# Moving steps in four written-out lists, one fixed sequence for a reciprocal root, and an early Silu, in an encoder block on one core

## Chip, cores and metric

The kernel runs on one core of one Trainium2 chip. Its time is the device time of one launch in microseconds (us). Three runs were made of it; the number that counts is their median.

## What is computed

One layer of an encoder on 256 tokens of width 2048, in float32. h = RMSNorm(x) goes through one projection that gives queries, keys and values of three token mixers A, B and C and three gates of width 2048. Each mixer's result goes through its own branch projection; the gates merge the three; an output projection w_o and a residual add follow; then a SwiGLU feed-forward (FFN) of inner width 5632.

```python
h = rms_norm(x, g_mix)
proj = h @ w_in                      # q, k, v of A and B, q of C, 3 gates
oa, ob, oc = dilated_attention(...), grouped_query_attention(...), cross_attention(mem, ...)
gates = sigmoid(gt)
merged = gates[0] * (oa @ w_br_a) + gates[1] * (ob @ w_br_b) + gates[2] * (oc @ w_br_c)
x = x + merged @ w_o
hf = rms_norm(x, g_ffn) @ w_ffn_in
x = x + (silu(hf[..., :D_FF]) * hf[..., D_FF:]) @ w_ffn_out
```

## The kernel before, in words

**Products in two halves.** Every weight block is a tile of 128 x 1024 float32 ("raw", 512 KB, one DMA of SP's queue, issued in `load`, L207). ScalarE rounds it to the matmul type (the high half, `whi`, L418), VectorE subtracts that from the block (the low half, `wlo`, L428), and each product is three matmuls: high by high, high by low, low by high. All matmuls are recorded at L79, where a helper issues them.

**Stages.** First the projection of the memory tokens and eight projections of q, k and v (`product`), with the attention worked between them as side jobs; then gates and branches (`merging`, pairs of 512 columns), the output projection (`projecting`) and the FFN (`feeding`), in which eleven pairs of hidden columns alternate with the pairs of the second FFN matrix. From `merging` on, all pairs run as one stream through `run(everything(), 4)`.

**A pair and its steps.** `pair` computes two 512-column blocks (c = 0 and 1) for 256 tokens (two halves t = 0 and 1). For most of the inner dimension it uses a scheme with seven products in place of eight (`seventh`, L537). Its four sums stand in four PSUM banks, called Y and X (c = 0) and W and Q (c = 1); in the first gate pair (`early`) a bank V takes the place of X as a result. The steps of a pair are written out by hand as a string:

- l and r load the blocks of one double step (`begin`, `begin2`); `begin` loads b11 and t and has GpSimd's queue (POOL, L503) add a further block into t.
- X, W, P, Y, Q, Z, H are the seven products, 6 matmuls each, with the number of the double step behind the letter (0 or 1). X adds to bank X, W and Z to bank W, Y to bank Y, P and Q to bank X again, H to X (or V). P, Q and H first make their block on VectorE (L549, L551, L553).
- d and D are plain products over a whole block of 256 inner rows, for c = 0 (banks Y and X, or V) and c = 1 (banks W and Q): 12 matmuls.
- A dot takes one step from the list that the pair before has left over.

Each entry has three lists: front (with dots), back, and the left-over end that goes to the next pair.

**The turning points of the chain** are in `phase_end` (L514): when the last X is done, ScalarE copies bank X into Y (L526); when the last W is done, ScalarE copies bank W away as m5 (L529); when the last P is done, VectorE writes W = m5 - X (L531); when the last Q is done, VectorE writes Q = m5 - X (L535), and in the `early` pair ScalarE first copies X to `u` (L521) and VectorE adds it to V (L522).

**What sets the order.** `run` prepares four steps ahead of the one whose matmuls it issues: a step's `ready` issues its load, its block sum, its high half and (one step later, `low(1)`) its low half; `products` issues its matmuls. The matmuls and SP's DMAs keep program order. `nc.follow` puts an instruction behind the one that was last given to it on the same engine, so the high halves on ScalarE and the low halves, block sums and bank operations on VectorE each form one fixed sequence. An engine works through its own queue in order, so an instruction that waits holds those behind it. Whatever is not given to `nc.follow` is placed by the planner, which simulates the program and takes what is ready, by priority. Side jobs are generators which `tick` moves on after every step's products, one at most each time; `urgent` gives theirs a high priority.

**The reciprocal root.** `row_scale` (L153) turns a row's sum of squares into r = 1/sqrt(mean + eps): one `tensor_scalar` (L156), then `rsqrt` (L138) with a shift and a subtraction on the bits (L142, L143) and three Newton rounds of three operations (L147 to L149), then a copy (L158) and a square (L159). In `projecting` the job `later` (L910) squares the sums on ScalarE (L914) and, at the last of four column blocks, reduces them (L918) and calls `row_scale` for r_f. The first use of r_f is the scale of the Silu of the first FFN pair (`hidden`, L947). That Silu reads banks W and Q, which the next pair's W0 needs.

**Activation tables.** ScalarE loads a table before the first function that is not in the one that it has: at the start (L338, a copy on the two-column tile `two`), before the first Sigmoid (L814) and before the first Silu (L947).

Of the kernel before, what the change touches and what calls it, by code (L numbers as in the profile page):

```python
# [13 lines left out]
I32 = mybir.dt.int32  # L14
AF = mybir.ActivationFunctionType
ALU = mybir.AluOpType
AX = mybir.AxisListType
# [4 lines left out]
D = 2048  # L22
# [9 lines left out]
EPS = 1e-6  # L32
# [19 lines left out]


STEPS_GATE = [
# [3 lines left out]
STEPS_O = ("l0 X0 . r0 W0 . P0 Y0 . Q0 .", "Z0 D2 H0 D3 d2 D6 d3 D7 D4 D5", "d6 d7 d4 d5")  # L58
STEPS_O2 = ("l0 X0 . r0 W0 . P0 Y0 . Q0 .", "Z0 D2 H0 D3 d2 D4 D5 d3 D6 D7", "d4 d5 d6 d7")
STEPS_FFN0 = ("l0 l1 X0 X1 . r0 W0 . r1 W1 . P0 P1 . Y0 Y1 Q0 Q1", "Z0 Z1 D6 H0 D7 H1 D4 D5", "d6 d7 d4 d5")  # L60
STEPS_FFN = ("l0 l1 X0 X1 . r0 W0 r1 W1 P0 P1 . Y0 Y1 . Q0 Q1 .", "Z0 Z1 D4 H0 D5 H1 D6 D7", "d4 d5 d6 d7")
STEPS_LAST = ("l0 l1 X0 X1 . r0 W0 . r1 W1 . P0 P1 . Y0 Y1 Q0 Q1", "Z0 Z1 H0 H1 D4 D5", "d4 d5")
STEPS_LAST2 = ("l0 l1 X0 X1 . r0 W0 r1 W1 P0 P1 . Y0 Y1 Q0 Q1", "Z0 Z1 D4 H0 D5 H1 d4 d5", "")


class InOrder:
# [37 lines left out]
def encoder_block(ctx: ExitStack, tc: tile.TileContext, a: dict, out: bass.AP):  # L104
    nc = InOrder(tc)
# [13 lines left out]
    def s8(shape, name, dt=F32R, pool=None):  # L119
        return (pool or big).tile(shape, dt, name=name, tag="s8")  # L120

    def s4(shape, name, dt=F32):
        return mid.tile(shape, dt, name=name, tag="s4")
# [14 lines left out]
    def rsqrt(v, shape):  # L138

        y = small.tile(shape, F32, name="rs_y")  # L140
        h = small.tile(shape, I32, name="rs_h")
        nc.vector.tensor_scalar(h, v.bitcast(I32), 1, None, op0=ALU.logical_shift_right)  # L142
        nc.vector.tensor_scalar(y.bitcast(I32), h, -1.0, float(0x5F3759DF), op0=ALU.mult, op1=ALU.add)  # L143
        for _ in range(3):
            t = small.tile(shape, F32, name="rs_t")
            y2 = small.tile(shape, F32, name="rs_y")
            nc.vector.scalar_tensor_tensor(t, y, -0.5, y, op0=ALU.mult, op1=ALU.mult)  # L147
            nc.vector.tensor_mul(t, t, v)
            nc.vector.scalar_tensor_tensor(y2, t, 1.5, y, op0=ALU.add, op1=ALU.mult)  # L149
            y = y2  # L150
        return y

    def row_scale(ss, r):  # L153

        v = small.tile([P, T], F32, name="rs_v")
        nc.vector.tensor_scalar(v, ss, 1.0 / D, EPS, op0=ALU.mult, op1=ALU.add)  # L156
        y = rsqrt(v, [P, T])
        nc.vector.tensor_copy(r[:, 0], y)  # L158
        nc.vector.tensor_mul(r[:, 1], y, y)  # L159


    side, now = [], [0]
# [11 lines left out]
    def start(steps):  # L174

        job = [0, steps]
        side.append(job)
        advance(job)
# [7 lines left out]
    def urgent(steps):  # L186

        while True:
            with tc.high_priority():
                try:  # L190
                    lag = next(steps)
                except StopIteration:
                    return
            yield lag
# [91 lines left out]
    def transposed(src, dst, g=None, lag=1, also=None):  # L286


        full = None
        for h in range(2):  # L290
            if h:
                yield lag
            tp = bank("tp", "tp")
            for k in range(2):
                for t in range(T):
                    nc.tensor.transpose(tp[:, k * S + t * P:k * S + (t + 1) * P],
                                        src[t][:, (2 * h + k) * P:(2 * h + k + 1) * P], ident)
            if g is None:
                d = dst(2 * h, 2)
                split(d[0], d[1], tp.rearrange("p (k s) -> p k s", s=S))  # L300
            else:
                for k in range(2):
                    d = dst(2 * h + k, 1)
                    split(d[0], d[1], tp[:, k * S:(k + 1) * S], g(2 * h + k))
            if also is not None:
                if full is None:
                    full = s4([P, 2, 4, P], "ffull")
                to, of = full[:, :, 2 * h:2 * h + 2], tp.rearrange("p (k t s) -> p k t s", t=T, s=P)
                if g is None:
                    nc.scalar.activation(to, of, AF.Copy)  # L310
                else:
                    for k in range(2):
                        nc.scalar.activation(to[:, k], of[:, k], AF.Copy, scale=g(2 * h + k))
        if also is not None:
            token_sums(full, also)
# [20 lines left out]
    two = const.tile([P, 2], F32, name="two")  # L336
# [288 lines left out]
    def take_slots(ps, slots, r, name="x"):  # L625
# [22 lines left out]
        if n:  # L648
# [4 lines left out]
            nc.vector.tensor_mul(ss[:, :, :n], ss[:, :, :n], each(1))  # L653
            nc.vector.tensor_scalar(v[:, :, :n], ss[:, :, :n], 1.0 / HD, EPS, op0=ALU.mult, op1=ALU.add)
            nc.vector.tensor_mul(f[:, :, :n], rsqrt(v[:, :, :n], [P, T, n]), each(0))
            yield EVAC_LAG
            for t in range(T):
# [178 lines left out]
    ss1 = const.tile([P, T, 4], F32, name="ss1")  # L836
# [55 lines left out]
    def projecting():  # L892
        def rows():
            yield 16
            for t in range(T):
                x.append(s8([P, D], f"x{t}", F32))
                nc.sync.dma_start(out=x[t], in_=a["x"][t * P:(t + 1) * P, :])
                yield 1
        start(rows())
        mTl = lambda k: (mT[k // 4][:, 0, k % 4], mT[k // 4][:, 1, k % 4])  # L900
        ended = []
        for n in (0, 2):
            def add(c, r, n=n):
                xc = [x[t][:, (n + c) * NC:(n + c + 1) * NC] for t in range(T)]
                for t in range(T):
                    nc.vector.tensor_add(xc[t], r[t], xc[t])
                ended.append(n + c)
                last = len(ended) == 4

                def later():  # L910
                    yield 1
                    sq = s4([P, T, NC], "sq")
                    for t in range(T):
                        nc.scalar.activation(sq[:, t], xc[t], AF.Square, accum_out=ss1[:, t, n + c:n + c + 1])  # L914
                    if last:
                        yield 1
                        ssr = small.tile([P, T], F32, name="ss", bufs=1)
                        nc.vector.tensor_reduce(ssr, ss1, axis=AX.X, op=ALU.add)  # L918
                        row_scale(ssr, r_f)
                    yield 2  # L920
                    if not x1T:
                        x1T.extend(s8([P, 2, 4, S], "x1T") for _ in range(4))
                        room.extend(form_room(3))
                    yield from transposed(xc, lambda k, m: (x1T[n + c][:, 0, k], x1T[n + c][:, 1, k]),
                                          lambda k: gT[:, 2, 4 * (n + c) + k:4 * (n + c) + k + 1], 2,
                                          also=room[2 + n + c] if n == 0 else None)
                start(urgent(later()))
            yield pair(block_pair(a["w_o"], n), mTl, STEPS_O2 if n else STEPS_O, add, TWO[:1], by_room(lambda: room))
# [6 lines left out]
    def feeding():  # L935
        for c0, c1 in ((0, 4), (4, 8), (8, KF // 4)):
# [3 lines left out]
            for n in range(c0, c1):  # L940
                av = []

                def hidden(c, v, av=av, n=n - c0, hT=hT):
# [8 lines left out]
                    def later():  # L952
                        tl = hT[n] = s8([P, 2, 4, S], "hT", pool=home(n))
                        yield 3
                        yield from transposed([av[0][:, t] for t in range(T)],
                                              lambda k, m: (tl[:, 0, k:k + m], tl[:, 1, k:k + m]), lag=2,
                                              also=room[n] if n < 2 else None)
                    start(urgent(later()))
                yield pair(lambda u, c, n=n: a["w_ffn"][n][2 * u + 1 - c], x1l, STEPS_FFN if n else STEPS_FFN0, hidden,
                           TWO, by_room(lambda: room[2:]))  # L960
            pairs = (STEPS_LAST, STEPS_LAST2) if last else (STEPS_FFN, STEPS_FFN)
            for n in (0, 2):
# [105 lines left out]
```

## Time and profile before

| | us |
|---|---|
| three runs | 1372.01, 1372.15, 1373.7 |
| median | 1372.15 |
| the profiled execution | 1372.53 |
| its span, first to last instruction | 1370.8 |
| TensorE busy in it | 1356.7 (99%) |
| VectorE busy | 1156.3 (84%) |
| ScalarE busy | 856.8 (63%) |
| table loads, starting at | 1.2, 283.6, 714.6 |

The granted clock of TensorE over the whole execution was 0.997. Two kinds of views are used below. Timeline rows tell when an instruction started, how long it took, its engine (PE is TensorE, DVE VectorE, ACT ScalarE), its line, what it writes and reads, and in square brackets how long the engine was idle before it and what ended that. Window rows tell, for a stretch of time, how long each engine was busy, how many instructions that were, and the granted clock.

### The profile page before, as it was taken

How to read it: one execution, taken by the hardware profiler on the slowest of the kernel's cores; microseconds unless marked ns; L12 is line 12 of the kernel's file. 1: busy time of each engine (PE TensorE's matmuls, PEld its weight loads, DVE VectorE, ACT ScalarE, POOL GpSimd, SP SyncE). 2: the span in 40 equal slices, each digit the busy share in tenths (PEclk: the TensorE clock that was granted, in tenths of full speed). 3: DMA queues.
4: the chain of work that ended last, by engine and by line, in shares of the span. 5: the costliest groups of instructions: out<-in, count | busy, mean ns of one | idle time of the engine just before them, and what ended most of it. 6: DMA issues, size and time to landing. Idle time of an engine off the chain costs nothing.

```text
span 1370.8 us, 17289 instructions
## 1 busy us (share of the span) xinstructions
PE 1356.7 (99%) x6170; PEld 1122.8 (82%) x6170; DVE 1156.3 (84%) x1412; ACT 856.8 (63%) x1110; POOL 53.2 (4%) x60
## 2 busy tenths in 40 slices
PE   9999999998999999999999999999999999999998
PEld 7878888887878888888878888888888888888887
DVE  6878877767879779878888998889999889989997
ACT  7776666655656556656666666655666656566664
POOL 0010000000000000000000000000000000000000
PEclk9999999999999999999999999999999999999999
DMA  9976455555586594775477666786666786666873
GB/s 366 342 237 210 139 153 183 156 171 202 196 291 198 180 314 156 258 265 168 166 246 226 193 226 204 252 265 217 212 219 213 247 275 194 213 224 216 276 214 107
DMA packets 86343, 301.18 MB, mean 220 GB/s; under 512 B 9777, under 2 KB 12337, under 8 KB 86001
## 3 DMA queue, kind: packets, MB, share of 16 engines
q1 hardware_dynamic: 79488, 275.94, 57.6%
q0 software_dynamic: 6624, 24.12, 9.5%
q8 instruction: 48, 0.79, 0.2%
q14 instruction: 39, 0.31, 0.1%
q10 hardware_dynamic: 144, 0.02, 0.0%
HBM read 297.17 MB, written 2.88 MB: 219 GB/s over the span
## 4 chain that ended last, share of the span: by engine, by line
PE 94%; DVE 3%; DMA 1%; issue 1%; ACT 1%; SPq 0%; DVEq 0%; ACTq 0%; POOLq 0%
PE mmX L79 28%; PE mmW L79 20%; PE mmY L79 15%; PE mm L79 15%; PE mmQ L79 11%; DVE wlo L428 1%; PE tp L79 1%; DMA raw<-in_w_gate 1%; PE sc L79 1%; PE o L79 1%; PE mmV L79 1%; PE pT L79 1%; PE hT L79 0%; DMA raw<-in_w_mem 0%; ACT whi L418 0%
## 5 line engine op out<-in xcount | busy, mean ns | idle before, releaser
L418 ACT ACTIVATE whi<-raw 128x1024 fp32r<-128x1024 f32 (+1 forms) x364 | 379.3, 1054 | 232.4 <-DVE raw L551 54.9
L428 DVE TENSOR_TENSOR wlo<-raw,whi 128x1024 fp32r<-128x1024 f32 (+1 forms) x364 | 438.2, 1218 | 74.2 <-ACT whi L418 70.5
L79 PE MATMUL mm<-whi,xT 128*128 128x512 f32 x640 | 202.9, 393 | 0.1
L418 ACT ACTIVATE whi<-more 128x1024 fp32r<-128x1024 f32 x100 | 105.2, 1058 | 63.6 <-DVE more L553 24.9
L428 DVE TENSOR_TENSOR wlo<-more,whi 128x1024 fp32r<-128x1024 f32 x100 | 122.0, 1221 | 26.8 <-ACT whi L418 24.2
L133 DVE TENSOR_TENSOR wlo<-raw,whi 128x1024 fp32r<-128x1024 f32 x82 | 103.0, 1258 | 44.8 <-ACT whi L132 43.6
L79 PEld LDWEIGHTS mm<-whi,xT 128*128 128x128 f32 x640 | 119.5, 188 | 24.2 <-DVE V L136 0.5
L428 DVE TENSOR_TENSOR wlo<-both,whi 128x1024 fp32r<-128x1024 f32 x89 | 108.7, 1222 | 31.6 <-ACT whi L418 30.6
L418 ACT ACTIVATE whi<-both 128x1024 fp32r<-128x1024 f32 x89 | 94.0, 1056 | 59.9 <-PE mmQ L79 21.0
L132 ACT ACTIVATE whi<-raw 128x1024 fp32r<-128x1024 f32 x82 | 86.8, 1061 | 67.9 <-PE mm L79 52.7
L79 PE MATMUL mmW<-whi,forms 128*128 128x512 f32 x368 | 123.7, 395 | 3.3 <-ACT av L947 3.3
L79 PE MATMUL mm<-wlo,xT 128*128 128x512 f32 x320 | 125.8, 393 | 0.0
L79 PE MATMUL mmX<-whi,forms 128*128 128x512 f32 x368 | 122.0, 391 | 0.0
L79 PE MATMUL mmX<-whi,x1T 128*128 128x512 f32 x352 | 120.9, 389 | 0.0
L79 PE MATMUL mmY<-whi,x1T 128*128 128x512 f32 x264 | 88.9, 389 | 0.0
L79 PEld LDWEIGHTS mmW<-whi,forms 128*128 128x128 f32 x368 | 70.1, 190 | 18.4 <-ACT av L947 3.7
L79 PEld LDWEIGHTS mmX<-whi,forms 128*128 128x128 f32 x368 | 69.1, 188 | 14.3
L79 PEld LDWEIGHTS mmX<-whi,x1T 128*128 128x128 f32 x352 | 66.1, 188 | 13.7
L79 PE MATMUL mmW<-wlo,forms 128*128 128x512 f32 x184 | 72.5, 394 | 0.0
L79 PE MATMUL mmX<-wlo,forms 128*128 128x512 f32 x184 | 71.6, 389 | 0.0
L79 PEld LDWEIGHTS mm<-wlo,xT 128*128 128x128 f32 x320 | 60.2, 188 | 12.2 <-issue 0.7
L79 PE MATMUL mmX<-wlo,x1T 128*128 128x512 f32 x176 | 68.5, 389 | 0.0
(276 smaller groups left out, 2597.1 us busy)
## 6 DMA issues: line engine op xcount, KB each, us to landing
raw<-in_w_ffn SPq DMA_DIRECT2D x122, 512.0 KB, 6.0
raw<-in_w_gate SPq DMA_DIRECT2D x67, 512.0 KB, 5.0
raw<-in_w_qkv SPq DMA_DIRECT2D x64, 512.0 KB, 4.1
raw<-in_w_ffn_out SPq DMA_DIRECT2D x55, 512.0 KB, 6.2
both<-in_w_ffn SPq DMA_DIRECT2D x28, 512.0 KB, 6.2
more<-in_w_ffn SPq DMA_DIRECT2D x26, 512.0 KB, 9.7
raw<-in_w_o SPq DMA_DIRECT2D x21, 512.0 KB, 4.3
more<-in_w_ffn_out SPq DMA_DIRECT2D x18, 512.0 KB, 6.8
```

The lines of the kernel that those rows point to most:

```text
L79: ins = op(*args, **kw)
L132: nc.scalar.activation(hi, src, AF.Copy)
L133: nc.vector.tensor_sub(lo, src, hi.bitcast(F32))
L418: nc.follow(nc.scalar.activation(hi[:, o], v, AF.Copy))
L428: nc.follow(nc.vector.tensor_sub(*due.pop(0)))
```

## The change

Three things are changed.

1. In the first list of STEPS_GATE, d4 goes from behind X1 to behind W1, and d6 from before Z0 to behind Z1. In the second list of STEPS_GATE and in STEPS_FFN0, STEPS_LAST and STEPS_LAST2, Y1 goes from before Q0 to behind Q1.
2. All operations of `rsqrt` and `row_scale`, and the reduction L918 before them, are given to `nc.follow`. Only in the stream of pairs does `nc.follow` do anything, so this concerns r_f.
3. Behind the Squares of the last block of `projecting`, a Silu of one column of the tile `two` into its other column is issued.

```diff
 STEPS_GATE = [
-    ("l0 l1 X0 X1 d4 r0 W0 r1 W1 P0 P1 d5 Y0 Y1 Q0 Q1 d6 Z0 Z1", "H0 D4 H1 D5 D6 D7", "d7"),
-    ("l0 l1 X0 . . X1 r0 W0 r1 W1 P0 P1 . Y0 Y1 Q0 Q1", "Z0 Z1 H0 D4 H1 D5 D6 D7", "d4 d5 d6 d7"),
+    ("l0 l1 X0 X1 r0 W0 r1 W1 d4 P0 P1 d5 Y0 Y1 Q0 Q1 Z0 Z1 d6", "H0 D4 H1 D5 D6 D7", "d7"),
+    ("l0 l1 X0 . . X1 r0 W0 r1 W1 P0 P1 . Y0 Q0 Q1 Y1", "Z0 Z1 H0 D4 H1 D5 D6 D7", "d4 d5 d6 d7"),
...
-STEPS_FFN0 = ("l0 l1 X0 X1 . r0 W0 . r1 W1 . P0 P1 . Y0 Y1 Q0 Q1", "Z0 Z1 D6 H0 D7 H1 D4 D5", "d6 d7 d4 d5")
+STEPS_FFN0 = ("l0 l1 X0 X1 . r0 W0 . r1 W1 . P0 P1 . Y0 Q0 Q1 Y1", "Z0 Z1 D6 H0 D7 H1 D4 D5", "d6 d7 d4 d5")
...
-STEPS_LAST = ("l0 l1 X0 X1 . r0 W0 . r1 W1 . P0 P1 . Y0 Y1 Q0 Q1", "Z0 Z1 H0 H1 D4 D5", "d4 d5")
-STEPS_LAST2 = ("l0 l1 X0 X1 . r0 W0 r1 W1 P0 P1 . Y0 Y1 Q0 Q1", "Z0 Z1 D4 H0 D5 H1 d4 d5", "")
+STEPS_LAST = ("l0 l1 X0 X1 . r0 W0 . r1 W1 . P0 P1 . Y0 Q0 Q1 Y1", "Z0 Z1 H0 H1 D4 D5", "d4 d5")
+STEPS_LAST2 = ("l0 l1 X0 X1 . r0 W0 r1 W1 P0 P1 . Y0 Q0 Q1 Y1", "Z0 Z1 D4 H0 D5 H1 d4 d5", "")
...
-        nc.vector.tensor_scalar(h, v.bitcast(I32), 1, None, op0=ALU.logical_shift_right)
+        nc.follow(nc.vector.tensor_scalar(h, v.bitcast(I32), 1, None, op0=ALU.logical_shift_right))
...
-            nc.vector.tensor_mul(t, t, v)
+            nc.follow(nc.vector.tensor_mul(t, t, v))
...
-        nc.vector.tensor_copy(r[:, 0], y)
+        nc.follow(nc.vector.tensor_copy(r[:, 0], y))
...
                     if last:
+                        nc.scalar.activation(two[:, 1:], two[:, :1], AF.Silu)
                         yield 1
                         ssr = small.tile([P, T], F32, name="ss", bufs=1)
-                        nc.vector.tensor_reduce(ssr, ss1, axis=AX.X, op=ALU.add)
+                        nc.follow(nc.vector.tensor_reduce(ssr, ss1, axis=AX.X, op=ALU.add))
                         row_scale(ssr, r_f)
```

More of the change, by code (lines that the diff above doesn't have):

```diff
@@ L141, in rsqrt @@
         h = small.tile(shape, I32, name="rs_h")
-        nc.vector.tensor_scalar(h, v.bitcast(I32), 1, None, op0=ALU.logical_shift_right)
-        nc.vector.tensor_scalar(y.bitcast(I32), h, -1.0, float(0x5F3759DF), op0=ALU.mult, op1=ALU.add)
+        nc.follow(nc.vector.tensor_scalar(h, v.bitcast(I32), 1, None, op0=ALU.logical_shift_right))
+        nc.follow(nc.vector.tensor_scalar(y.bitcast(I32), h, -1.0, float(0x5F3759DF), op0=ALU.mult, op1=ALU.add))
         for _ in range(3):
@@ L146, in rsqrt @@
             y2 = small.tile(shape, F32, name="rs_y")
-            nc.vector.scalar_tensor_tensor(t, y, -0.5, y, op0=ALU.mult, op1=ALU.mult)
-            nc.vector.tensor_mul(t, t, v)
-            nc.vector.scalar_tensor_tensor(y2, t, 1.5, y, op0=ALU.add, op1=ALU.mult)
+            nc.follow(nc.vector.scalar_tensor_tensor(t, y, -0.5, y, op0=ALU.mult, op1=ALU.mult))
+            nc.follow(nc.vector.tensor_mul(t, t, v))
+            nc.follow(nc.vector.scalar_tensor_tensor(y2, t, 1.5, y, op0=ALU.add, op1=ALU.mult))
             y = y2
@@ L155, in row_scale @@
         v = small.tile([P, T], F32, name="rs_v")
-        nc.vector.tensor_scalar(v, ss, 1.0 / D, EPS, op0=ALU.mult, op1=ALU.add)
+        nc.follow(nc.vector.tensor_scalar(v, ss, 1.0 / D, EPS, op0=ALU.mult, op1=ALU.add))
         y = rsqrt(v, [P, T])
-        nc.vector.tensor_copy(r[:, 0], y)
-        nc.vector.tensor_mul(r[:, 1], y, y)
+        nc.follow(nc.vector.tensor_copy(r[:, 0], y))
+        nc.follow(nc.vector.tensor_mul(r[:, 1], y, y))
     side, now = [], [0]
```

## The prediction

> **What bounds the kernel now.** First the head of the page, then the waits of the matmul engine (engine, line, what it waited for: us in total, times, longest), then the chain of waits for the pace of matmuls.
>
> ```profile
> span 1370.8 us, 17289 instructions
> PE 1356.7 (99%) x6170; PEld 1122.8 (82%) x6170; DVE 1156.3 (84%) x1412; ACT 856.8 (63%) x1110; POOL 53.2 (4%) x60
> ```
>
> ```profile
> PE mmW L79 <- ACT av L947: 3.3, 1, 3.3
> PE mmY L79 <- ACT mmY L526: 2.6, 1, 2.6
> ...
> PE mmX L79 <- DVE mmQ L535: 1.1, 2, 0.6
> PE mmV L79 <- DVE mmV L522: 1.1, 1, 1.1
> PE mmW L79 <- DVE wlo L428: 0.5, 2, 0.3
> ```
>
> ```profile
> 409.27 2.72 PE mmX L79 x12
> ```
>
> TensorE sets the end. Twelve matmuls take 2.72 us, 0.227 each, and it almost never stops, so nothing can be gained but its few stops. A step of one letter with X, W, P, Y, Q, Z or H is 6 matmuls, 1.36 us; a step d or D is 12, 2.72. All large stops lie where the change works. The profiled execution took 1372.53 us (span 1370.8); the median of the runs is 1372.15, so 0.4 comes off at the end. About 0.2%, 2.7 us, is what a measurement of this kernel can tell from no change.
>
> **The first list of STEPS_GATE: d4.** Timeline rows: start, duration, engine, line, operation, and the engine's idle time before it with its cause.
>
> ```profile
> 316.88 0.39 PE L79 MATMUL mmY<-whi 128*128 128x512 f32 x1
> 319.84 0.50 PE L79 MATMUL mmY<-whi,xT 128*128 128x512 f32 x1 [2.57 <-ACT mmY L526]
> ```
>
> ```profile
> 318.25 1.06 ACT L418 ACTIVATE whi<-raw 128x1024 fp32r<-128x1024 f32 x1 [2.82 <-DVE raw L549]
> 319.21 0.58 ACT L526 ACTIVATE mmY<-mmX 128x512 f32<-128x512 f32 x1
> ```
>
> ```profile
> 321.20:324.50 3.30, 3.30 (x10) 2.52 (x9) 1.69 (x2) 0.63 (x2) 0.00 (x0) 0.50 0.00 0
> 717.10:720.40 3.30, 3.30 (x9) 2.59 (x8) 0.00 (x0) 1.08 (x2) 0.00 (x0) 0.50 0.34 137
> ```
>
> X1 ends at 317.1, and d4 adds to bank Y, which is first copied from X. That copy stands in ScalarE's fixed sequence behind the high half of P0, which waits for VectorE's sum L549; so it ends at 319.79, and TensorE stands from 317.11 to 319.84: 2.73 us. Then it runs at half clock: the window rows (third number from the right: granted clock) show 0.50 for 3.3 us, which loses 1.65. Together 4.4.
>
> By the change W0 and W1 run there: 317.11 + 2.72 = 319.83, just as the copy ends. The copy itself stays where it is: four steps are prepared ahead of the one that is multiplied, and these are the same four (d4, W0, W1, P0) in either order. On SP's queue d4's load goes behind the four of r0 and r1, still ahead of P0's need; POOL's sums into t (L503) are issued with l0 and l1, before either order differs. Z0 and Z1 load nothing, so d6's load keeps its place. The cover is exact: were the copy later, each us of it would come back. So the stop goes, and P0 comes at 322.6 instead of 327.07. What is late next is VectorE:
>
> ```profile
> 325.45 1.23 DVE L428 TENSOR_TENSOR wlo<-both,whi 128x1024 fp32r<-128x1024 f32 x1 [2.51 <-ACT whi L418]
> ```
>
> ```profile
> 340.40 0.69 DVE L535 TENSOR_TENSOR mmQ<-m,mmX 128x512 f32<-128x512 f32 x1
> ```
>
> This idle 2.51 is a wait for a buffer that d4 frees; by the new order W0 frees it earlier. Then VectorE's work down to the subtraction L535, which ended at 341.1, ends at 338.6 or earlier, and H0's low half, 1.1 us more, at 339.7. TensorE, from 322.6 over eight steps of 1.36 and two of 2.72, comes to H0 at 338.9 and uses that half at 339.1. VectorE also idled about 0.9 us between (behind Q1 and before Y0, where TensorE now comes earlier), so the two are about level: I charge 0.3 (0 to 0.6). Net 4.1.
>
> The Trainium skill ("TensorE: Matmul & The Clock Gate", "Why this matters for your kernels") lets the clock fall after idle gaps of over about 3 us. The trace disagrees: 2.57 us were enough here. By the page the 1.65 behind this first gap would have another cause and stay, and the total would be 1365.2.
>
> **The first list: d6.**
>
> ```profile
> 339.08 0.39 PE L79 MATMUL mmY<-whi,xT 128*128 128x512 f32 x1
> 340.54 0.50 PE L79 MATMUL mmV<-whi,xT 128*128 128x512 f32 x1 [1.07 <-DVE mmV L522]
> ```
>
> d6's second half goes to bank V, which must first take up X behind Q1 (copy L521, sum L522). 340.54 - 339.08 - 0.227 = 1.23 us. Behind Z0 and Z1 there are 2.72 us more of cover: all 1.2 goes, and the clock was not lost here.
>
> **Y1 behind Q1 in the other four lists.** The stops here are the waits for mmQ, L535, in the second gate pair and in STEPS_LAST.
>
> ```profile
> 383.91 0.47 PE L79 MATMUL mmX<-whi,xT 128*128 128x512 f32 x1 [0.57 <-DVE mmQ L535]
> ```
>
> ```profile
> 1310.44 0.70 DVE L531 TENSOR_TENSOR mmW<-m,mmX 128x512 f32<-128x512 f32 x1 [0.35 <-PE mmX L79]
> ```
>
> ```profile
> 361.50:383.80 22.30, 21.84 (x96) 17.58 (x95) 22.07 (x23) 13.21 (x15) 0.00 (x0) 1.00 0.33 103
> 1311.00:1331.20 20.20, 19.69 (x91) 15.84 (x90) 20.20 (x22) 12.44 (x13) 0.88 (x1) 1.00 0.92 259
> ```
>
> The subtraction for mmQ gets 1.36 us more of cover. But the windows (busy us of PE, PEld, DVE, ACT) show VectorE full before these stops: 22.07 of 22.30 and 20.20 of 20.20. H0 needs the same work of VectorE in either order, so what the subtraction no longer delays, H0's or H1's low half does. In the gate pair I take 0 of the 0.57 + 0.3 (the longest wait for wlo follows it, at D4) = 0.9 us (0 to 0.9). In STEPS_LAST the subtraction L531 idled VectorE for 0.35 while P1 ran; now Q1's sum goes ahead of it and fills that: 0.3, between 0 and its 0.5 (the 1.1 of the two waits for mmQ less 0.57). STEPS_LAST2 had no stop, but there the subtraction, 0.7 us like L531, moves ahead of D4's low half: a loss of 0.3, between 0 and its whole 0.7. STEPS_FFN0's own list is counted below. No DMA is issued by Y or Q; Q1 frees its buffer a step earlier.
>
> **The reciprocal root.** The first Silu needs r_f.
>
> ```profile
> 707.64 0.39 PE L79 MATMUL mmQ<-whi,x1T 128*128 128x512 f32 x1
> ...
> 713.09 0.39 PE L79 MATMUL mmX<-whi,x1T 128*128 128x512 f32 x1
> 716.73 0.52 PE L79 MATMUL mmW<-whi,forms 128*128 128x512 f32 x1 [3.25 <-ACT av L947]
> ```
>
> ```profile
> 714.63 1.28 ACT L947 ACT_TABLE_LOAD   x1
> 715.99 0.69 ACT L947 ACTIVATE av<-mmW,scales 128x512 f32<-128x512 f32 x1
> ```
>
> ```profile
> 691.24 0.15 DVE L918 TENSOR_REDUCE ss<-ss 128x2 f32<-128x8 f32 x1
> ...
> 715.79 0.16 DVE L158 COPY scales<-rs_y 128x2 f32<-128x2 f32 x1
> ```
>
> W0 of the second FFN pair needs a bank that Silu has to read. Banks W and Q were complete at 708.0, but Silu began at 715.99, right behind the copy of r_f (715.95): fifteen tiny operations took from 691.24, each one behind 1.2 us of other VectorE work. The table load ended at 715.91, no later than r_f, so taking it away alone would free nothing. The stop is 716.73 - 713.09 - 0.227 = 3.41, with the half clock at 717.1 another 1.65: 5.1 us.
>
> What the sequence costs in one piece, seen where one ran nearly so:
>
> ```profile
> 62.91 0.16 DVE L149 SCALAR_TENSOR_TENSOR rs_y<-rs_t,rs_y 128x2 f32<-128x2 f32 x1
> 63.11 0.17 DVE L158 COPY scales<-rs_y 128x2 f32<-128x2 f32 x1
> ...
> 695.77 1.22 DVE L428 TENSOR_TENSOR wlo<-more,whi 128x1024 fp32r<-128x1024 f32 x1
> ```
>
> ```profile
> 688.04 0.61 ACT L914 ACTIVATE sq<-x 128x512 f32<-128x512 f32 x1
> ```
>
> ```profile
> 698.35 0.39 PE L79 MATMUL mmW<-whi,x1T 128*128 128x512 f32 x1
> ```
>
> One such step takes 63.11 - 62.91 = 0.20 from start to start, as each waits for the one before, so fifteen (the last two side by side) take about 2.8 us. They are issued at Y0's products, which by the new list is behind Y1's low half and ahead of Z0's. r_f is then there by about 692, and even with a table load (1.28) and two Silus behind 708.0 the bank is free at 710.6, before the 713.3 at which W0 comes. So the whole 5.1 goes.
>
> The price is a wait in VectorE's fixed order: the sum of squares waits for ScalarE's second Square (688.04, 0.61 us), and behind it stand the low halves of Z0, Z1, D6, H0 and D7. The tightest is D7: its low half ended at 695.77 + 1.22 = 696.99 for a use one matmul behind 698.35, at 698.58, with 1.6 us in hand. 2.7 us of insertion (2.8, of which 0.1 lay there before) take that and 1.1 more; waiting for Square adds up to 1, and the idle moments that the new order fills give some back. I charge 1.5 (0 to 2.0).
>
> **The Silu on a two-column tile.** It depends on nothing but a constant and is in no fixed order. How the planner treats such an operation:
>
> ```profile
> 0.84 0.06 DVE L349 MEMSET relb<- 64x6 f32 x1
> ```
>
> ```profile
> 3.85 0.91 ACT L135 ACTIVATE memT<-rawT,gT 128x256 fp32r<-128x256 f32 x2 [1.18 <-DMA gT<-in_g_rows]
> ```
>
> This memset is written in a job that is held for ten steps, and it ran at 0.84 us. I expect the tiny Silu at the start as well, in ScalarE's 1.18 idle us before 3.85. Its load is then lost to the loads for Exp and Sigmoid: five loads instead of three, the late one still in front of L947, and nothing fetched ahead. At the start 0.3 us would move, behind which the first weights' DMA lands later anyway; I charge 0.2 for this and for what the planner shifts among the operations without fixed order (from 0.5 of loss to 0.4 of gain, as each of the stops in the waits of TensorE that stay is under 0.6).
>
> The Trainium skill ("ScalarE: Activation LUTs", "What ACT_TABLE_LOAD costs") gives 2.66 us for a switch, 1.38 of it a drain. The rows show 1.28 and Silu 0.08 later. By the page two more switches are 5.3 us of ScalarE and at most 1366 in total if half stays uncovered.
>
> **The sum.** 4.1 + 1.2 + 0 + 0.3 - 0.3 + 5.1 - 1.5 - 0.2 = 8.7. From 1372.5: 1363.8; less the 0.4 by which the profiled run is over the median: about 1363.5.
>
> **The rivals.**
> - More goes: VectorE's earlier start also clears the 0.9 of the gate pair and 0.5 of STEPS_LAST, the sequence hides, and the planner's shift gives 0.4. Best case 4.4 + 1.2 + 0.9 + 0.5 + 5.1 + 0.4 = 12.5 below 1372.15: 1359.7, up to 1361.5. Against it stand the full windows. 0.17.
> - The sequence blocks longer: the tiny Silu stays beside the Squares, so its load and itself (1.5 us of ScalarE) delay Square and the next high halves, and a stop of VectorE turns into one of TensorE over 2.57 us with 1.65 of half clock behind it. 1363.5 + 2 + 1.65 = 1367.2, range 1365.5 to 1368. Against it: the memset's row. 0.15.
> - Silu is still late: the planner sets it behind high halves that wait for TensorE, as at 714.6. 3.4 + 1.65 come back: 1368.5. For it: ScalarE's row of 715.99; against it: r_f is there some 24 us earlier. 0.05.
> - Slower: two more table loads and a Silu at the head of ScalarE's queue make the planner lay the operations without fixed order anew in the first 300 us (attention on top of the qkv products), where TensorE stands nowhere now. A stop there of over 2.57 us costs 2.7 + 1.65 = 4.4; from three such on the gain of 8.7 is overdrawn by more than the 2.7: 1376.7. Against it: loads of 1.28 on an engine that is busy 63%. 0.04; two of them, no change, 1372.3: 0.05.
>
> **How the numbers follow.** The forecast's own case, 1362 to 1365.5, has 0.54. The range that leaves 2 in 10 out goes from the best case to the middle of the second rival: 1359.7 to 1367.5. Faster by over 0.2% are the forecast and the first three rivals, 0.91; within it 0.05; slower 0.04.
>
> **What would show it.** Right: no wait of mmY for L526 and none of mmW for L947; the granted clock at 1.00 throughout; fifteen small operations in a row on VectorE near 689 to 692, with a short stop of TensorE between Z0 and D7; H0 of the second gate pair still waiting for VectorE; five table loads, one in the first 5 us. Wrong: a table load near 688, a new stop before 300 us, Silu behind 713, or P0 to H0 of the first gate pair with stops over 0.6.

## The result and the profile after

| | before | changed |
|---|---|---|
| median | 1372.26 (4 runs) | 1365.08 (4 runs) |
| lowest to highest | 1372.01 to 1373.7 | 1364.67 to 1366.68 |
| the profiled execution, its span | 1372.53, 1370.8 | 1364.67, 1362.9 |

The ratio is 0.9948, with a 95% interval from 0.993 to 0.9965: 7.2 us faster, about 0.5%. The forecast was 1363.5 in a range of 1359.7 to 1367.5. What follows is read at the same places as before the change.

The page of the changed kernel, then what TensorE waited for in it:

```profile
span 1362.9 us, 17306 instructions
PE 1352.8 (99%) x6170; PEld 1119.7 (82%) x6170; DVE 1156.5 (85%) x1412; ACT 858.8 (63%) x1113; POOL 53.2 (4%) x60
```

```profile
PE mmW L79 <- DVE wlo L428: 4.1, 4, 2.3
PE idle L79 <- POOL ident masks.py:199: 1.4, 1, 1.4
PE mmY L79 <- DVE wlo L428: 0.2, 1, 0.2
```

Of the five waits that the prediction began with, four are gone: for the Silu, for the copy into Y, for mmV and for mmQ. The fifth has grown, the one for VectorE's low halves: 0.5 us in two before, now 4.1 in four. (The wait for `ident` lies in the first two us.) ScalarE has three instructions more: the Silu and two table loads.

**Where d4 stood.** Timeline rows of TensorE and of ScalarE's copy into Y, then the window behind (PE, PEld, DVE, ACT, POOL, granted clock, share and rate of the DMAs):

```profile
319.13 0.39 PE L79 MATMUL mmW<-whi,forms 128*128 128x512 f32 x1
319.36 0.40 PE L79 MATMUL mmY<-whi,xT 128*128 128x512 f32 x1
...
318.61 0.58 ACT L526 ACTIVATE mmY<-mmX 128x512 f32<-128x512 f32 x1
```

```profile
320.30:323.60 3.30, 3.30 (x16) 2.75 (x15) 3.23 (x4) 3.30 (x5) 0.00 (x0) 1.00 0.35 140
```

d4 follows W1 at the pace of matmuls, 0.23 behind it, and the clock is whole where it had been 0.50. The copy ended at 319.19, 0.17 before d4 began: the cover was as exact as the prediction had it.

**What came late next in the two gate pairs.** First TensorE, then VectorE ahead of the first of these stops:

```profile
339.87 0.40 PE L79 MATMUL mmW<-whi,xT 128*128 128x512 f32 x1
340.88 0.50 PE L79 MATMUL mmW<-wlo,xT 128*128 128x512 f32 x1 [0.62 <-DVE wlo L428]
...
377.82 0.40 PE L79 MATMUL mmX<-whi,xT 128*128 128x512 f32 x1
378.29 0.51 PE L79 MATMUL mmX<-wlo,xT 128*128 128x512 f32 x1
...
379.56 0.40 PE L79 MATMUL mmW<-whi,xT 128*128 128x512 f32 x1
380.56 0.50 PE L79 MATMUL mmW<-wlo,xT 128*128 128x512 f32 x1 [0.60 <-DVE wlo L428]
```

```profile
338.47 1.22 DVE L553 TENSOR_TENSOR more<-raw,more 128x1024 f32<-128x1024 f32 x1
339.61 2.52 DVE L428 TENSOR_TENSOR wlo<-more,whi 128x1024 fp32r<-128x1024 f32 x2
```

The stop at D4 of the first pair is new: 340.88 - 339.87 - 0.227 = 0.78. D4's low half is the first of the two in VectorE's last row; it could start only at 339.61, behind H1's block sum, and D4 wanted it at 340.10. In the second pair there are two such stops, 0.24 at H0 (378.29 - 377.82 - 0.227) and 0.77 at D4; there VectorE had been full before, and still is (busy 16.60 of the 16.60 us from 361.50 to 378.10).

**The first FFN pair,** where the root's sequence now runs. TensorE, then VectorE, then the window behind the first stop:

```profile
685.52 0.40 PE L79 MATMUL mmW<-whi,forms 128*128 128x512 f32 x1
688.26 0.50 PE L79 MATMUL mmW<-wlo,forms 128*128 128x512 f32 x1 [2.34 <-DVE wlo L428]
...
691.35 0.40 PE L79 MATMUL mmW<-whi,x1T 128*128 128x512 f32 x1
692.26 0.50 PE L79 MATMUL mmW<-wlo,x1T 128*128 128x512 f32 x1 [0.52 <-DVE wlo L428]
```

```profile
680.65 0.68 DVE L906 TENSOR_TENSOR x<-mmX,x 128x512 f32<-128x512 f32 x1
683.12 0.16 DVE L919 TENSOR_REDUCE ss<-ss 128x2 f32<-128x8 f32 x1 [1.79 <-ACT sq L914]
...
684.84 0.48 DVE L136 SCALAR_TENSOR_TENSOR x1T<-tp,gT,x1T 128x256 fp32r<-128x256 f32 x1 [0.36 <-ACT x1T L135]
...
686.92 0.15 DVE L159 TENSOR_TENSOR scales<-rs_y 128x2 f32<-128x2 f32 x1
686.99 1.22 DVE L428 TENSOR_TENSOR wlo<-more,whi 128x1024 fp32r<-128x1024 f32 x1
```

```profile
688.40:691.70 3.30, 3.30 (x16) 2.43 (x16) 3.30 (x4) 0.53 (x1) 0.00 (x0) 1.00 0.91 258
```

VectorE is done with L906 at about 681.3, waits 1.8 for the second Square, then works off the fifteen small operations with two of x1T between them, and only at 686.99 begins Z0's low half. TensorE stands at Z0 (688.26 - 685.52 - 0.227 = 2.51) and again at D6 (0.68). With the first matmuls behind each stop 0.1 late, that is 3.4 us. The clock stays whole.

**The Silu.** Rows of ScalarE at the start and before the first use of r_f, and of TensorE where W0 of the second FFN pair begins:

```profile
2.69 1.28 ACT L916 ACT_TABLE_LOAD   x1
...
704.33 1.28 ACT L948 ACT_TABLE_LOAD   x1
705.63 0.69 ACT L948 ACTIVATE av<-mmW,scales 128x512 f32<-128x512 f32 x1
```

```profile
710.99 0.39 PE L79 MATMUL mmX<-whi,x1T 128*128 128x512 f32 x1
711.22 0.39 PE L79 MATMUL mmW<-whi,forms 128*128 128x512 f32 x1
```

The two-column Silu went to the start, its table was lost, and a load stands before the true Silu as ever. But that Silu now reads its bank at 705.63, 5.6 us ahead of W0, which runs on without a stop.

The ledger, in us (half clock as lost time: half of the 3.3 us window; stops that no row here shows are differences of two starts in the trace, less 0.227):

| place | before | changed | forecast gain |
|---|---|---|---|
| first gate pair, d4 | 2.73 + 1.65 | 0 | 4.4 |
| first gate pair, D4 | 0 | 0.8 + 0.1 | -0.3 |
| first gate pair, d6 | 1.23 | 0 | 1.2 |
| second gate pair, H0 and D4 | 0.74 + 0.49 | 0.25 + 0.77 | 0 |
| last pair but one | 0.7 | 0 | 0.3 |
| last pair | 0 | 0.24 | -0.3 |
| second FFN pair, Silu | 3.41 + 1.65 | 0 | 5.1 |
| first FFN pair, sequence | 0 | 3.4 | -1.5 |

The measured gains add up to 4.4 - 0.9 + 1.2 + 0.2 + 0.7 - 0.2 + 5.1 - 3.4 = 7.1, beside the 7.2 of the medians. The two profiled executions, from which the rows come, differ by more: 1370.8 - 1362.9 = 7.9. Of that, 0.4 has arisen in the first 7 us (the first matmul with a low half starts at 6.65 before and at 6.29 after); most of the rest is the 0.1 by which the first matmuls behind the stops that went had been late. The forecast column lacks the 0.2 that was charged for the early Silu.

### The profile page after: what moved, and what is told of

Read it like the earlier page. It is cut to its first block, busy times and chain, and to the rows that moved or that the text cites. A ratio compares the mean times of both kernels' runs of the same rounds, so it can differ in the third digit from the quotient of the medians.

```text
span 1362.9 us, 17306 instructions
## 1 busy us (share of the span) xinstructions
PE 1352.8 (99%) x6170; PEld 1119.7 (82%) x6170; DVE 1156.5 (85%) x1412; ACT 858.8 (63%) x1113; POOL 53.2 (4%) x60
## 4 chain that ended last, share of the span: by engine, by line
PE 96%; DVE 2%; issue 0%; DMA 0%; ACT 0%; SPq 0%; DVEq 0%
PE mmX L79 29%; PE mmW L79 20%; PE mm L79 16%; PE mmY L79 16%; PE mmQ L79 11%; DVE wlo L428 1%; PE tp L79 1%; PE sc L79 1%; PE o L79 1%; PE pT L79 1%; PE hT L79 0%; PE mmV L79 0%; DMA raw<-in_w_mem 0%; DVE raw L551 0%; DVE more L553 0%
## 5 line engine op out<-in xcount | busy, mean ns | idle before, releaser
L418 ACT ACTIVATE whi<-raw 128x1024 fp32r<-128x1024 f32 (+1 forms) x355 | 369.8, 1054 | 230.0 <-PE mmQ L79 50.0
L428 DVE TENSOR_TENSOR wlo<-raw,whi 128x1024 fp32r<-128x1024 f32 (+1 forms) x355 | 427.7, 1218 | 79.7 <-ACT whi L418 76.5
L79 PEld LDWEIGHTS mm<-whi,xT 128*128 128x128 f32 x640 | 119.5, 188 | 24.2 <-DVE V L136 0.5
L418 ACT ACTIVATE whi<-both 128x1024 fp32r<-128x1024 f32 x99 | 104.2, 1057 | 55.6 <-PE mmQ L79 20.6
L428 DVE TENSOR_TENSOR wlo<-both,whi 128x1024 fp32r<-128x1024 f32 x99 | 120.5, 1221 | 16.0 <-ACT whi L418 14.8
```

Source lines behind the costliest of these rows:

```text
L79: ins = op(*args, **kw)
L418: nc.follow(nc.scalar.activation(hi[:, o], v, AF.Copy))
L428: nc.follow(nc.vector.tensor_sub(*due.pop(0)))
```

## The experiments

Each was timed in five rounds beside the kernel before on the same chip; times are medians, and the ratio is to the kernel before, with its 95% interval. The changed kernel was not timed beside them. The kernel before has medians from 1371.76 to 1373.04 in the four series, so a difference between kernels of different series is sure to about 1 us, and smaller ones are decided by the traces. Four kernels first, each with one part of the change alone.

| kernel | median | ratio |
|---|---|---|
| d4 and d6 alone | 1367.22 | 0.9962 (0.995 to 0.9975) |
| Y1 behind Q1 alone, four lists | 1371.54 | 0.9994 (0.9985 to 1.0003) |
| the root's sequence alone | 1370.09 | 0.9984 (0.9975 to 0.9993) |
| the early Silu alone | 1372.21 | 1.0003 (0.9994 to 1.0011) |
| the kernel before beside them (27 runs) | 1372.24 | |

**1. d4 and d6 alone.**

```diff
-    ("l0 l1 X0 X1 d4 r0 W0 r1 W1 P0 P1 d5 Y0 Y1 Q0 Q1 d6 Z0 Z1", "H0 D4 H1 D5 D6 D7", "d7"),
+    ("l0 l1 X0 X1 r0 W0 r1 W1 d4 P0 P1 d5 Y0 Y1 Q0 Q1 Z0 Z1 d6", "H0 D4 H1 D5 D6 D7", "d7"),
```

> The kernel before with d4 and d6 of the first list of STEPS_GATE moved, and nothing else. Theory (the stops add up, each where it was read): the stop at d4 with its half clock (2.73 + 1.9, in the trace of after gone) and the one at d6 (1.2 + 0.1) go, and the stop at D4 of the same pair that the trace of after shows (PE waits for the low half, 0.8 + 0.1) comes in: 4.65 + 1.35 - 0.9 = 5.1 below the kernel before, about 1367.2; the Silu's wait at the second FFN pair and its half clock stay as before. Rival (the D4 stop belongs to the early Silu or to something else that the planner re-placed): no stop at D4, 6.0 below, 1366.3. Rival (the half clock is not caused by the stop): 0.50 for about 3.3 us is still found somewhere near 320 to 325 us, and only 3.2 goes, 1369.

Measured: 5.0 us. D4's stop is there without any other part of the change, and the waits of the root are untouched:

```profile
339.91 0.40 PE L79 MATMUL mmW<-whi,xT 128*128 128x512 f32 x1
340.92 0.50 PE L79 MATMUL mmW<-wlo,xT 128*128 128x512 f32 x1 [0.61 <-DVE wlo L428]
```

So the stop at D4 is the price of this list, and the list carries most of the whole gain.

**2. Y1 behind Q1 alone.** The four lists as in the change, the root unpinned.

> The kernel before with Y1 behind Q1 in the second list of STEPS_GATE, STEPS_FFN0, STEPS_LAST and STEPS_LAST2, and nothing else; the root's operations stay without order. Theory (VectorE is the bound at both turning points, and the loss in the first FFN pair belongs to the fixed sequence): 0.2 gained in the second gate pair, 0.75 in the last pair but one, 0.25 lost in the last pair, nothing in the first FFN pair: 0.7 below, about 1371.5, and the stop of 5 us at the Silu stays. Rival (the loss in the first FFN pair comes from Y1's new place, which takes one step of cover from Z0's low half): 2 to 3 us of stops between Z0 and D7 of the first FFN pair here too, and the time is 1.5 to 2.5 above the kernel before, about 1374.

Measured: 0.7 us, as the theory has it, but its interval includes no change; the trace decides. It has no stop over 0.15 us between 640 and 712, so the list does not by itself cost anything in the first FFN pair.

**3. The root's sequence alone.** `nc.follow` around the reduction, `rsqrt` and `row_scale`; all lists and the missing Silu as before.

> The kernel before with the reduction and the root's operations given to the fixed sequence, and nothing else; Y1 stays ahead of Q0 in all lists. Theory (the sequence alone takes the Silu's stop away, and itself costs 3.4 as read in the trace of after): 5.1 gained, 3.4 lost, about 1370.5; three table loads, the one before the first Silu still late (near 705) and harmless. Rival (Y1's new place is what makes the sequence dear): the stop between Z0 and D7 is 0.3 to 0.8, and the time is 1367.5 to 1368. Rival (the table must be there early): the wait for the Silu stays at 1.3 or more, and the time is over 1371.

Measured: 2.15 us, with three table loads, the last at 707.0, and no wait for the Silu. So the sequence alone takes the stop of 5.1 away, and its own cost is there without Y1's move. TensorE's rows at its d4 and in the first FFN pair, and the window behind its d4:

```profile
316.18 0.39 PE L79 MATMUL mmY<-whi 128*128 128x512 f32 x1
319.14 0.50 PE L79 MATMUL mmY<-whi,xT 128*128 128x512 f32 x1 [2.57 <-ACT mmY L526]
...
688.70 0.40 PE L79 MATMUL mmW<-whi,forms 128*128 128x512 f32 x1
691.45 0.50 PE L79 MATMUL mmW<-wlo,forms 128*128 128x512 f32 x1 [2.35 <-DVE wlo L428]
```

```profile
319.10:322.40 3.30, 3.26 (x14) 2.73 (x15) 3.09 (x3) 1.23 (x2) 0.00 (x0) 1.00 0.00 0
```

There is one stop of 2.52 (691.45 - 688.70 - 0.227) and none at D6. And behind the same d4 stop as in the kernel before the clock is whole here: see experiments 10 and 11 and the last section.

**4. The early Silu alone.**

> The kernel before with the Silu on the two-column tile, and nothing else. Theory (it floats to the head of ScalarE's queue and its table is lost to the next function): five table loads, the second before 5 us, the late one near 714 still there, the same stops: 1372.2, no difference over 0.3. Rival (it is fetched ahead after all, or it moves other operations without fixed order): the load before the late Silu is gone, or stops before 300 us change; 0.5 or more on either side.

Measured: no difference. Five table loads, at 1.2, 2.7, 119.5, 284.0 and 716.4. The profiled execution has a longer stop before W0 (3.99 instead of 3.41); over all runs nothing is left of it.

The four parts add up to 5.0 + 0.7 + 2.15 + 0 = 7.9, 0.7 more than the change brings. By itself that proves nothing, as each part's interval is more than 1 us to either side. But in the first FFN pair the sequence alone has one stop and the change has two, and the second, at D6, is 0.7. Experiment 12 takes that up; the size of the sequence's cost comes first.

**5. The root's sequence two steps later.**

```diff
                         nc.scalar.activation(two[:, 1:], two[:, :1], AF.Silu)
-                        yield 1
+                        yield 3
```

> The changed kernel with the root's sequence issued two steps later (behind the subtraction L535 in VectorE's order), all else the same. Theory (the mis-sized cost of the sequence is VectorE's wait of 1.8 us for the second Square, in front of the fifteen operations): the reduction waits no more, the sequence of about 3.3 us with one x1T operation in it stands ahead of D6's low half, which had 1.6 us less in hand: stops of 1.7 in place of 3.4, so 1363.4. Rival (the fifteen operations themselves with what is mixed into them are the cost, and the wait lies beside it): still 3 or more, 1365.

Measured: 1365.67, ratio 0.9952 (0.9939 to 0.9964), no better than the change. The theory fell. VectorE, then TensorE at D6:

```profile
687.25 0.48 DVE L136 SCALAR_TENSOR_TENSOR x1T<-tp,gT,x1T 128x256 fp32r<-128x256 f32 x1 [1.12 <-ACT x1T L135]
...
688.82 1.22 DVE L553 TENSOR_TENSOR raw<-raw,raw 128x1024 f32<-128x1024 f32 x1
```

```profile
687.93 0.40 PE L79 MATMUL mmW<-whi,x1T 128*128 128x512 f32 x1
691.23 0.50 PE L79 MATMUL mmW<-wlo,x1T 128*128 128x512 f32 x1 [2.90 <-DVE wlo L428]
```

The wait for Square is gone, the reduction starting without one at 684.19, but the sequence with its x1T operations, one of which waits 1.12 us for ScalarE, still holds VectorE until 688.82: 4.6 us in one piece. TensorE stands 3.07 us at D6, and this execution then ran at half clock for 3.41 us, which is in its time too.

**6. The same fifteen operations, spread.** They stay in VectorE's fixed order, but a job issues one behind each of four steps and two behind each later one.

```diff
-                        nc.follow(nc.vector.tensor_reduce(ssr, ss1, axis=AX.X, op=ALU.add))
-                        row_scale(ssr, r_f)
+                        start(urgent(spread(row_steps(ssr, r_f))))
...
+    def spread(ops):
+        for k, ins in enumerate(ops):
+            nc.follow(ins)
+            if k < 4 or k % 2:
+                yield
```

> The changed kernel with the root's fifteen operations still in VectorE's fixed order, but one of them behind each of four steps and two behind each later step, in place of all in one piece. Theory (it is the one piece that costs): the reduction still waits 1.8 us for the second Square, but Z0's low half then comes at 684.5, ahead of its use at 685.7; D7's low half comes up to 0.7 late; stops of 0 to 0.8 in place of 3.4, r_f ready near 700, still ahead of the Silu: 1362.4 (1361.6 to 1363). Rival (the wait for Square is the cost): 1.8 of stops stay, 1363.5 or more. Rival (r_f now late for the Silu): a wait of mmW for the Silu's line of over 1, 1365 and more.

Measured: 1361.67, ratio 0.9925 (0.9911 to 0.9938): 3.4 us below the change, as much as its two stops with what follows them. TensorE has no stop over 0.15 us between 640 and 720. VectorE at the same place:

```profile
683.51 0.16 DVE L896 TENSOR_REDUCE ss<-ss 128x2 f32<-128x8 f32 x1 [1.79 <-ACT sq L940]
683.59 1.22 DVE L428 TENSOR_TENSOR wlo<-more,whi 128x1024 fp32r<-128x1024 f32 x1
```

The wait of 1.79 for Square is still there and costs nothing, as Z0's low half comes next instead of fourteen operations. Neither wait nor operations are the cost by themselves; the unbroken piece is. The last operation of the root that the Silu needs starts at 700.87, early enough. (A stop of 0.67 in the last pair, in place of 0.24 in the changed kernel, is not explained by any run here.)

**7. D4 ahead of H0, and D5 ahead of H1, in the first two gate pairs,** on the changed kernel.

```diff
-    ("l0 l1 X0 X1 r0 W0 r1 W1 d4 P0 P1 d5 Y0 Y1 Q0 Q1 Z0 Z1 d6", "H0 D4 H1 D5 D6 D7", "d7"),
-    ("l0 l1 X0 . . X1 r0 W0 r1 W1 P0 P1 . Y0 Q0 Q1 Y1", "Z0 Z1 H0 D4 H1 D5 D6 D7", "d4 d5 d6 d7"),
+    ("l0 l1 X0 X1 r0 W0 r1 W1 d4 P0 P1 d5 Y0 Y1 Q0 Q1 Z0 Z1 d6", "D4 H0 D5 H1 D6 D7", "d7"),
+    ("l0 l1 X0 . . X1 r0 W0 r1 W1 P0 P1 . Y0 Q0 Q1 Y1", "Z0 Z1 D4 H0 D5 H1 D6 D7", "d4 d5 d6 d7"),
```

> The changed kernel with D4 ahead of H0 and D5 ahead of H1 in the back lists of the first and the second gate pair (D needs one operation of VectorE, H two), all else the same. Theory (the stops left there are low halves that are late because H0's sum and low half stand ahead of D4's): the 0.9 in the first pair and 1.1 of the 1.2 in the second go: 2.0 below the changed kernel, 1363.1. Rival (VectorE is full, so that the same stop turns up at H0 or D5): 1365 as before.

Measured: 1363.84, ratio 0.994 (0.9928 to 0.9953): 1.2 below the change, which the intervals do not tell apart. By the trace, half of the theory holds. In the first pair the stop is gone. In the second it has moved:

```profile
377.83 0.39 PE L79 MATMUL mmW<-whi,xT 128*128 128x512 f32 x1
378.98 0.50 PE L79 MATMUL mmW<-wlo,xT 128*128 128x512 f32 x1 [0.76 <-DVE wlo L428]
```

0.92 us at D4 in its earlier place: there VectorE is the bound, as the rival said.

**8. All that helped, together:** the spread root, D4 ahead of H0, the old STEPS_LAST2, no early Silu.

> The changed kernel with the root's operations spread over the steps, D4 ahead of H0 and D5 ahead of H1 in the first two gate pairs, the old list of STEPS_LAST2, and without the early Silu. Theory (the parts add): 2.7 + 2.0 + 0.25 below the changed kernel, 1360.2; no stop over 0.8 us behind 20 us, the clock at 1.00 in every run and the runs within 1 us of each other; three table loads. Rival (VectorE's full stretches give the stops back elsewhere): 1362 or more.

Measured: 1359.47, ratio 0.9911 (0.9897 to 0.9925): 5.6 below the change, faster than both kernels. Its four runs lie between 1359.11 and 1360.51, a little wider than the 1 us expected, all with the clock at 1.000. There are three table loads, and besides the one for `ident` this is left of TensorE's waits over 0.3 (the longer lies in the first 11 us):

```profile
PE mmW L79 <- DVE wlo L428: 1.1, 2, 0.8
```

**9. The table truly fetched ahead,** in the changed kernel.

```diff
-                        nc.scalar.activation(two[:, 1:], two[:, :1], AF.Silu)
+                        nc.follow(nc.scalar.activation(two[:, 1:], two[:, :1], AF.Silu))
```

> The changed kernel with the early Silu given to ScalarE's fixed sequence, so that it stays behind the high half that was issued last and its table is really fetched ahead; all else the same. Theory (the table's load was not what the second FFN pair waited for, once r_f is early: bank W is free near 707 and needed near 711.7): three loads, the last near 679, in ScalarE's idle 1.6 us there; none at the late Silu, and no gain: 1365.1 (1364.7 to 1366.5, if the load delays the second Square, and with it the sequence). Rival (the fetch is worth its load): 1.3 below the changed kernel, 1363.8.

Measured: 1365.57, ratio 0.9953 (0.994 to 0.9965): no gain. Three loads, the last one early:

```profile
678.33 1.28 ACT L916 ACT_TABLE_LOAD   x1
```

It cost nothing in ScalarE's idle time and saved nothing behind it. This execution has the same stop at Z0 as the changed kernel (2.52), but loses the clock behind it:

```profile
689.80:693.10 3.30, 3.30 (x11) 2.73 (x10) 3.25 (x4) 1.86 (x2) 0.00 (x0) 0.51 0.80 287
```

and has no stop at D6, since TensorE at half clock arrives there later.

**10 and 11. The stop and the clock.** The kernel of experiment 8 with d4 back behind X1, and with d4 behind W0: one stop of 2.73 or of half of that.

```diff
-    ("l0 l1 X0 X1 r0 W0 r1 W1 d4 P0 P1 d5 Y0 Y1 Q0 Q1 Z0 Z1 d6", "D4 H0 D5 H1 D6 D7", "d7"),
+    ("l0 l1 X0 X1 d4 r0 W0 r1 W1 P0 P1 d5 Y0 Y1 Q0 Q1 Z0 Z1 d6", "D4 H0 D5 H1 D6 D7", "d7"),
```

```diff
-    ("l0 l1 X0 X1 r0 W0 r1 W1 d4 P0 P1 d5 Y0 Y1 Q0 Q1 Z0 Z1 d6", "D4 H0 D5 H1 D6 D7", "d7"),
+    ("l0 l1 X0 X1 r0 W0 d4 r1 W1 P0 P1 d5 Y0 Y1 Q0 Q1 Z0 Z1 d6", "D4 H0 D5 H1 D6 D7", "d7"),
```

> The last kernel (spread root, D4 ahead of H0, without the early Silu) with d4 of the first list back behind X1, so that it has one large stop, of 2.73 us. Theory (the half clock is set off by this stop, for a time that differs from run to run): 2.7 above that kernel in every run, and 0 to 3 more by the clock: median 1364.0, the runs spread over 1.5 us or more, the granted clock 0.997 to 1.00 and each run longer by what its clock takes. Rival (the half clock has another cause): 1362.2, all runs within 1 us, the clock at 1.00.

> The same kernel with d4 behind W0, which covers half of the copy: one stop of 1.37 us. Theory (a stop of that size does not lose the clock, as the one of 1.23 at d6 did not): 1.4 above, 1360.9, the clock at 1.00 and the runs within 1 us. Rival (each large stop loses it, in proportion): 1361.8 or more, spread over 1 us or more.

Measured: 1363.45 (1362.69 to 1363.87) and 1360.67 (1360.36 to 1361.04); ratios 0.9937 (0.9923 to 0.995) and 0.9918 (0.9904 to 0.9931). The stop and the window behind it, of 10 and then of 11:

```profile
319.33 0.50 PE L79 MATMUL mmY<-whi,xT 128*128 128x512 f32 x1 [2.57 <-ACT mmY L526]
```

```profile
319.50:322.80 3.30, 3.30 (x9) 2.61 (x10) 2.88 (x3) 1.06 (x1) 0.00 (x0) 0.55 0.00 0
```

```profile
319.88 0.50 PE L79 MATMUL mmY<-whi,xT 128*128 128x512 f32 x1 [1.09 <-ACT mmY L526]
```

```profile
319.90:323.20 3.30, 3.30 (x15) 2.73 (x16) 3.25 (x4) 2.23 (x3) 0.00 (x0) 1.00 0.03 12
```

The long stop costs 4.0 over the kernel of experiment 8: 2.7 of stop, and by difference 1.3 of clock. The short one costs 1.2, no more than itself. Experiment 8 was of another series; by the ratios the two costs are 3.6 and 1.0. So the half clock belongs to the long stop. The five runs with the long stop spread over 1.2 us, less than the 1.5 expected, with clocks from 0.998 to 1.000.

**12. The old list of STEPS_FFN0 in the changed kernel** (Y1 ahead of Q0 in that list alone).

> The changed kernel with the old front list of STEPS_FFN0 (Y1 ahead of Q0), all else the same. Theory (behind the sequence, Y1's new place has D6's low half wait for one operation of VectorE more; this is the 0.7 by which the four parts alone add up to more than the change): one stop of 2.5 between Z0 and D7 and none of 0.7 at D6: 0.8 below the changed kernel, 1364.3. Rival (the list makes no difference there, and the 0.7 is scatter): both stops, 1365.1.

Measured: 1364.6, ratio 0.994 (0.9926 to 0.9954): 0.5 below the change, which the intervals do not tell apart. The stop at D6 is gone, and L535 stands behind D6's low half (690.06, against 691.19) where in the changed kernel it stood ahead of it (689.26, against 690.99). But this execution ran at half clock before D6, which hides such a stop too. The cleaner evidence is two other traces with the clock whole there: experiment 3, with the old list, has one stop only, and experiment 7, with the new list, has both, 2.52 at Z0 and 0.69 at D6. That Y1's place costs 0.7 at D6 once the sequence stands before it is likely, not shown by a time.

## Why the prediction was right, point by point

- **d4 and d6: right.** Both stops went; alone the list brings 5.0, where 4.1 + 1.2 were forecast.
- **D4's stop: mis-sized, 0.9 for 0.3** (bound 0.6). The prediction compared VectorE and TensorE at H0's low half and called them level. That one held TensorE up by less than 0.1; behind it in VectorE's sequence stood H1's block sum, and then D4's low half, which was not followed up.
- **Second gate pair and last pair: right** in sign and size (0.2 for 0, -0.24 for -0.3): with VectorE full, the stop moves to the next low half. **Last pair but one:** 0.7 in place of 0.3, over the bound of 0.5; the whole stop went.
- **The Silu's stop: right,** with its reason: r_f was the late one, not the table. Experiment 3 shows it with the load still at the late place.
- **The cost of the fixed sequence: this is the term that was mis-sized most, 3.4 for 1.5 (0 to 2.0).** The forecast took D7 as the tightest, with 1.6 in hand, against 2.7 of insertion and up to 1 for Square. What failed is the length of the piece. VectorE was held from 681.3 to 686.99, 5.7 us: 1.8 for Square, and 3.9 for the fifteen operations and two of x1T that run between them without being in the sequence, one waiting itself. With a piece of that length the next low half behind it is late already: Z0's would have ended at 681.3 + 1.2 = 682.5, for a use at 685.75, with 3.2 in hand. 5.7 - 3.2 = 2.5, the stop that was seen; D6 came on top. Experiment 6 shows that the piece is the cost. A bit of luck is in the result as well: the stop of 2.51 kept the clock in the profiled execution, where the same stop lost it in those of experiments 9 and 12, and the forecast had put no half clock behind it.
- **The early Silu: right,** to the start, five loads, no effect. The prediction's signs held too, except that the stop between Z0 and D7 was not short: 2.5 at Z0 and 0.7 at D6.
- **Against the Trainium skill** ("TensorE: Matmul & The Clock Gate", "Why this matters for your kernels"), which lets the clock fall after gaps of over about 3 us: the rows of experiment 10 have 0.55 behind an idle 2.57, as the prediction held; in experiment 3 the same idle time kept it. By the page's rule the prediction gave 1365.2, which lies close to the result, but not for that rule's reason: the window at 320.30 of the changed kernel shows that the half clock at d4 did go. The fixed 1.65 a stop was too simple all the same, as the last section shows.

Of the 1.6 us between forecast and result, the sequence makes 1.9 and D4 0.6; the last two pairs, the second gate pair and the Silu, which was charged with 0.2, give about 0.8 back.

## What to carry to other kernels

Fifteen tiny dependent operations pinned in one piece cost the in-order engine their sum and every wait that is met inside it; spread over the steps behind which they stand, the same operations in the same fixed order stopped TensorE nowhere in that pair, while left unpinned they were done more than 20 us later than in one piece. When a stop is to be taken away, the next one is found by following the bounding engine's sequence past the first user: for each low half, the time at which it ends less the time at which it is wanted, as far as the shortest. Before a table is fetched ahead, look at which of the waits ends last: here it was the scale, and the load was free wherever it stood.

## What the hardware showed that was not expected

**The half clock is not a fixed price; it depends on where a stop falls.** Behind the same stop of 2.73 at d4 the half clock lasted 3.41 us in the kernel before, with Y1's move alone and in experiment 10, 6.83 us with the early Silu alone, and it did not come with the root's sequence alone: from nothing to about 3 us lost. Stops of 2.5 went both ways (whole in the changed kernel, half in experiments 9 and 12); those of 1.3 and less, at d6 in four traces and in experiment 11 among them, never lost it.

The traces show what divides them. In the kernel before, the two stretches at half clock begin at 321.12 and 717.07, which is 395.95 us or 116 times 3.413 apart, and each lasts 3.41. In all 14 traces the stretches behind stops last one or two such periods and begin on a grid of this pitch, which lies differently in every execution. Each row here is one period of the grid, first of experiment 10, then of experiment 3; both have the same idle time of 2.57 at d4:

```profile
316.45:319.86 3.41, 0.84 (x4) 0.49 (x3) 3.38 (x3) 1.54 (x2) 0.00 (x0) 1.00 0.27 107
319.86:323.27 3.41, 3.41 (x9) 2.65 (x8) 2.52 (x3) 1.06 (x1) 0.00 (x0) 0.50 0.00 0
...
314.31:317.72 3.41, 2.26 (x10) 1.53 (x9) 3.38 (x5) 0.59 (x2) 0.00 (x0) 1.00 0.77 303
317.72:321.13 3.41, 1.99 (x9) 1.66 (x10) 3.32 (x4) 2.43 (x3) 0.00 (x0) 1.00 0.01 2
321.13:324.54 3.41, 3.41 (x17) 2.83 (x16) 2.32 (x2) 2.00 (x2) 0.00 (x0) 1.00 0.00 0
```

In experiment 10 the whole stop lies in one period, TensorE is busy for 0.84 us of it, and the next period runs at half clock. In experiment 3 the grid cuts the stop in two, TensorE is busy for 2.26 and 1.99, and the clock stays whole. The same holds in all 14 traces behind their first 10 us: a period at whole clock in which TensorE was busy for 1.47 us or less was followed by half clock in all eleven cases, one with 1.74 or more never. What happens between 1.47 and 1.74 is not known, and no run moved a stop against the grid on purpose.

This also fits the spread of the times: the 27 runs of the kernel before, with two long stops, reach from 1369.95 at a clock of 0.999 to 1374.02 at 0.996; those of the kernel of experiment 8, with none, differ by 1.4 us.

**A table load is no longer than its row.** The load at 704.33 took 1.28 and Silu began at 705.63, 0.02 behind it. The Trainium skill ("ScalarE: Activation LUTs", "What ACT_TABLE_LOAD costs") has 1.38 us of drain beside it; no run here shows that.
